# Opening of a two-layer DiT kernel: first scale and constants on other DMA queues, chunks loaded in pairs, modulation columns by transposes and a VectorE sum

## The chip, the cores and the metric

The kernel runs on one core of a Trainium2 chip. The time is the device time of one execution in microseconds; lower is better. All arithmetic is in float32, with matrix products made of three passes over a high and a low part of each operand (`hi` and `lo`, type fp32r).

## The reference, cut to what matters

```python
silu_c, silu_cc = jax.nn.silu(c), jax.nn.silu(c_ctx)
# layer 0
mod   = silu_c  @ ada_w[0] + ada_b[0]        # [1, 6*1024]
mod_c = silu_cc @ ada_w[0] + ada_b[0]
sh1, sc1, g1, sh2, sc2, g2 = jnp.split(mod, 6, axis=-1)     # sh1c, sc1c, ... likewise
h  = x   * (1.0 + sc1)  + sh1                # x:   256 tokens x 1024
hc = ctx * (1.0 + sc1c) + sh1c               # ctx: 256 tokens x 1024
p  = h @ ret_w_in[0]                         # [1024, 6144]: q, k, v, gates of 4 heads; hc likewise
# ... retention over h and hc, layer norms, MLP 1024 -> 4096 -> 1024, then a second layer
# with neighbourhood attention; the output is x, 256 x 1024
```

Only the first step concerns us: the two vectors `sh1` and `sc1` (and those of the context) come from a product with the first 2048 columns of `ada_w[0]`, and only with them can x and ctx be modulated and projected.

## The kernel before, in words

The opening works in eight **chunks** of 128 channels (k = 0 to 7). For chunk k it needs 128 columns of `ada_w[0]` for the shift (i = 0) and 128 for the scale (i = 1), each [1024 x 128], 512 KB, in rows of 512 B; the 128 columns of x and of ctx, 128 KB each, in rows of 512 B; and 128 rows of `ret_w_in[0]` for the q of head 0 (256 columns, 128 KB) and its v (512 columns, 256 KB). `chunk_loads(k)` issues them all on the SyncE queue (SP), in this order. The tile names in the trace are `rawq` (ada_w), `R` (x and ctx) and `raw` (weights).

For each chunk:
- `chunk_sums(k, i)`: TensorE multiplies the ada_w columns by the silu columns `cT`; the sums of eight row blocks land in four groups of 32 partitions of a PSUM bank (`pada`), in two accumulating rounds.
- `chunk_turn(k)`: TensorE transposes the four 128x128 tiles of x and ctx (`pt`, and the second half of the `pada` bank).
- `ws[k].high()`: ScalarE makes the high part of the weights; `ws[k].low()`: VectorE makes the low part.
- `chunk_row(k)`: VectorE copies the sums to SBUF (`row`).
- `chunk_columns(k)`: two float32 matmuls with a selector (`sel4`) add the four partial rows and turn them into columns; VectorE adds the bias (`mod`).
- `chunk_modulate(k)`: ScalarE and VectorE write the modulated high part `hTh`, then the unrounded value `aff`; VectorE subtracts to get the low part `hTl`.
- `chunk_q` and `part_v`: TensorE accumulates q (`pq`) and v (`pv`) over the chunks: 18 matmuls of 512 columns a chunk.

The loop of round k prepares chunk k+1 while it multiplies chunk k. TensorE, VectorE and ScalarE run in the order written out by hand here (their `on` flag is set before the first `turn_over`), and SP always does. So the order on each engine is the order of the code: in round k TensorE does the q and v products with `hTh` of chunk k, the sums and transposes of k+1, `part_v(k, 1, 0)` with `hTl`, the columns of k+1, and `part_v(k, 0, 1)`. From chunk 4 on, `low()` stands ahead of the columns on VectorE; before that, it stands between the two halves of `chunk_modulate`.

Beside the chunks, decay tables are made. In round 0, SP loads the distance table `dt` (192 KB) behind the chunks that were issued before the loop; in round 1 GpSimd makes three variants of it (`strip_tables`); and in rounds 2 to 5, behind `chunk_modulate`, `make_strip` puts four Exp on ScalarE and three operations on VectorE (tiles `e` and `strips`).

Ahead of all that, `turn_over(n)` issues n dummy matmuls (256 columns, operand `still`) that keep TensorE busy. `first_columns` transposes the 16 rows `crow` (c and c_ctx) with the identity in `cst0`, takes silu and spreads the result into `cT`; `first_biases` turns the bias rows `brow0`.

The order ahead of the loop:

```python
    turn_over(16)
    first_columns()
    turn_over(3)
    chunk_sums(0, 0)
    ...
    turn_over(1)
    first_biases()
    turn_over(3)
    chunk_sums(0, 1)
```

Arena slots: `AQ` names four slots of 8 KB a partition, one for each of the chunks in flight (both ada parts of a chunk share one slot). Weights of a chunk lie in a pool of four buffers.

Of the kernel before, what the change touches and what calls it, by code (L numbers as in the profile page):

```python
# [10 lines left out]
F32 = mybir.dt.float32  # L11
F32R = mybir.dt.float32r
AF = mybir.ActivationFunctionType
ALU = mybir.AluOpType
# [3 lines left out]
P = 128  # L18
D = 1024
KC = D // P  # L20
# [84 lines left out]
def kernel(  # L105
# [23 lines left out]
    pe, act, dve, pool, sp = (  # L129
        InOrder(tc, getattr(nc, e), e in PIN)  # L130
        for e in ("tensor", "scalar", "vector", "gpsimd", "sync")
    )
# [19 lines left out]
    def nm(s):  # L152
        uid[0] += 1
        return f"{s}_{uid[0]}"

    def bank(s="ps"):
        return psp.tile([P, 512], F32, tag="ps", name=nm(s))

    def slot(i, shape, dt, s):

        return arena.tile(shape, dt, tag=f"s{i}", name=nm(s))

    def scr(s, dt=F32):
        return scp.tile([P, 512], dt, tag="scr", name=nm(s))

    def tsl(t):
        return slice(t * P, (t + 1) * P)
# [125 lines left out]
    NC0 = P + 4  # L293
    cst0 = cpool.tile([P, NC0], F32, tag="cst0", name="cst0")
    cst1 = cpool.tile([P, CONSTS.shape[1] - NC0], F32, tag="cst1", name="cst1")
    crow = scr("crow")[:, :P]
    brow0 = scr("brow0")[:, :P]
    sp.dma_start(out=crow[0:8, :], in_=c.rearrange("a (k p) -> (a k) p", p=P))
    act.dma_start(out=crow[8:16, :], in_=c_ctx.rearrange("(k p) -> k p", p=P))
    act.dma_start(out=cst0[:], in_=consts[:, 0:NC0])  # L300
    act.dma_start(out=brow0[0:16, :], in_=ada_b[0][0 : 2 * D].rearrange("(r p) -> r p", p=P))

    def cv(name, p0=0, p1=P):
        o, w = CONST_COLS[name]
        if o < NC0:
            return cst0[p0:p1, o : o + w]
        return cst1[p0:p1, o - NC0 : o - NC0 + w]

    ident = cv("ident")
# [4 lines left out]
    bcol = cpool.tile([P, 2, KC], F32, tag="bcol", name="bcol")  # L314
# [4 lines left out]
    def first_columns():  # L319

        pc = bank("pc")
        pe.transpose(pc[:, 0:16], crow[0:16, :], ident[0:16, 0:16])
        act.activation(out=scol[:].rearrange("p a k -> p (a k)"), in_=pc[:, 0:16], func=AF.Silu)
        for t in range(2):
            dve.tensor_copy(
                out=cT[:, :, :, t], in_=scol[:, t, :].unsqueeze(2).broadcast_to([P, KC, 16])
            )

    def first_biases():

        pc = bank("pc")
        pe.transpose(pc[:, 0:16], brow0[0:16, :], ident[0:16, 0:16])
        for a in range(2):
            dve.tensor_scalar_add(out=bcol[:, a], in0=pc[:, 8 * a : 8 * a + 8], scalar1=float(a))

    def ln_rows():
        rows = scr("rows")[:, :P]
        sp.dma_start(out=rows[0:32, :], in_=ln_g.rearrange("l i (k p) -> (l i k) p", p=P))
        sp.dma_start(out=rows[32:64, :], in_=ln_b.rearrange("l i (k p) -> (l i k) p", p=P))
        for i, (l, w) in enumerate(COLUMNS):  # L340
            sp.dma_start(
                out=rows[64 + 16 * i : 80 + 16 * i, :],
                in_=ada_b[l][3 * w * D : (3 * w + 2) * D].rearrange("(r p) -> r p", p=P),
            )
        return rows
# [21 lines left out]
    mods = {}  # L367
# [353 lines left out]
    AQ = (S_GS, S_SH, S_SL, S_VH)  # L721
    adas, ws = {}, {}

    def chunk_ada(k):

        raw = slot(AQ[k % 4], [P, 2, KC, P], F32, "rawq")
        for i in range(2):
            w_ap = ada_w[0][:, i * D + P * k : i * D + P * k + P]
            sp.dma_start(out=raw[:, i], in_=w_ap.rearrange("(k p) n -> p k n", p=P))
        adas[k] = lambda i, kk: raw[:, i, kk, :]  # L730

    def chunk_x(k):
        cols = tsl(k)
        for a, src in enumerate((x, ctx_in)):
            sp.dma_start(out=RR[a][:, :, cols], in_=src[0][:, cols].rearrange("(t p) c -> p t c", p=P))

# [21 lines left out]
    def chunk_loads(k):  # L758
        chunk_ada(k)
        chunk_x(k)  # L760
        ws[k] = Weights(k)

    def turn_over(n):
        for _ in range(n):
            pe.matmul(pq[0][:, :256], lhsT=still[:, :P], rhs=still[:, :256], start=True, stop=True)
# [42 lines left out]
    prs, pts, rows = {}, {}, {}  # L808

    def chunk_sums(k, i):  # L810

        if k not in prs:
            prs[k] = bank("pada")
        for kk in range(KC):
            j = kk % 4
            pe.matmul(
                prs[k][32 * j : 32 * j + 32, tsl(i)],
                lhsT=cT[:, kk, :, :].rearrange("p a t -> p (a t)"),
                rhs=adas[k](i, kk),
                start=(kk < 4),  # L820
                stop=(kk >= 4),
                tile_position=(0, 32 * j),
            )

    def chunk_row(k, cols=slice(0, 2 * P)):
        if cols.start == 0:
            rows[k] = smp.tile([P, 256], F32, tag="row", name=nm("row"), bufs=1)
        dve.tensor_copy(out=rows[k][:, cols], in_=prs[k][:, cols])

    def chunk_columns(k):  # L830
        for i in range(2):
            pe.matmul(
                prs[k][:, 2 * i : 2 * i + 2], lhsT=rows[k][:, tsl(i)], rhs=cv("sel4")[:, 0:2],
                start=True, stop=True,
            )
        dve.tensor_add(
            out=mods[0, 0][:, :, k, :],
            in0=prs[k][:, 0:4].rearrange("p (s t) -> p s t", s=2),
            in1=bcol[:, :, k].unsqueeze(2).broadcast_to([P, 2, 2]),
        )  # L840
# [3 lines left out]
    def chunk_turn(k, ts=range(4)):  # L844

        if k not in pts:
            pts[k] = bank("pt")[:, 0:256], (prs[k][:, 256:512] if k else bank("pt")[:, 0:256])
        for t in ts:
            pe.transpose(pts[k][t // 2][:, tsl(t % 2)], R[t][:, tsl(k)], ident)
# [18 lines left out]
    def chunk_q(k, parts=((0, 0), (1, 0), (0, 1))):  # L868
        w, h = (ws[k].hi, ws[k].lo), hs(k, 0, NT)
        for a, b in parts:  # L870
            for dc in range(2):
                pe.matmul(
                    pq[dc][:], lhsT=w[a][:, tsl(dc)], rhs=h[b],
                    start=(k == 0 and a == b), stop=(k == KC - 1 and b == 1),
                )

    def part_v(k, a, b):
# [4 lines left out]
                start=(k == 0 and a == b), stop=(k == KC - 1 and b == 1),  # L882
            )

    act.dma_start(
        out=lgn[:, 0], in_=ret_decay[0].rearrange("(o d) h -> o (d h)", o=1).broadcast_to([P, 8])
    )
    for k in range(4):
        chunk_loads(k)
    for e in (act, dve, pe):  # L890
        e.on = True
    turn_over(16)
    first_columns()
    turn_over(3)
    chunk_sums(0, 0)
    chunk_row(0, tsl(0))
    turn_over(1)
    first_biases()
    turn_over(3)
    chunk_sums(0, 1)  # L900
    chunk_row(0, tsl(1))
    chunk_turn(0, (0, 1))
    chunk_columns(0)
    chunk_turn(0, (2, 3))
    turn_over(3)
# [9 lines left out]
    for k in range(KC):  # L915
        if k == 0:
            dt = slot(S_VL, [P, 4, 384], F32, "dt")
            sp.dma_start(out=dt[:, 0], in_=dist)
        if k == 3:
            sp.dma_start(out=cst1[:], in_=consts[:, NC0:])  # L920
            lrows = ln_rows()
        if k:
            chunk_q(k, ((0, 0),))
            part_v(k, 0, 0)
            chunk_q(k, ((1, 0), (0, 1)))
        if k < KC - 1:
            for i in range(2):
                chunk_sums(k + 1, i)
            chunk_turn(k + 1)
            ws[k + 1].high()  # L930
            chunk_row(k + 1)
            if k > 2:
                ws[k + 1].low()
        if k < 4:
            chunk_loads(k + 4)
        part_v(k, 1, 0)
        if k < KC - 1:
            chunk_columns(k + 1)
            chunk_modulate(k + 1, lambda: None if k > 2 else ws[k + 1].low())
        part_v(k, 0, 1)  # L940
        if k == 1:
            tabs = strip_tables(dt)
        if 1 < k < 6:
            make_strip(k - 2, *tabs)
        if k == KC - 1:
            ln_columns(lrows)
        if k > 5:
            take(0, 2 * (k - 5))
# [56 lines left out]
    for h in range(RH):  # L1005
# [9 lines left out]
        else:  # L1015
# [15 lines left out]
            for u in range(4):  # L1031
                ((wh, wl),) = take(1)
                for t in range(4):
                    for kk in range(2):
                        k = 2 * u + kk
# [72 lines left out]
        for t in range(4):  # L1108
            po = bank("po")
            scs = list(range(4)) if t < 2 else [2, 3]  # L1110
            for i, sc in enumerate(scs):
                a, b = S[sc]
# [5 lines left out]
            r = rstd_of(mv)  # L1118
            on = scr("on")[:] if t < 2 else gs[:, t, :]
            dve.tensor_scalar(  # L1120
                out=on, in0=po[:], scalar1=mv[:, 0:1], scalar2=r[:], op0=ALU.subtract, op1=ALU.mult
# [155 lines left out]
    for hf in range(2):  # L1277
# [65 lines left out]
        for half in range(2):  # L1343
# [39 lines left out]
            def settle(t):  # L1383

                add_to(t, 1, gated(pb[t], t, 1, G2), dve)
                stat(t, 1)
                return moments(t)
# [14 lines left out]
            m = settle(0)  # L1402
# [5 lines left out]
            m = settle(1)  # L1408
            mm2(2, 4, held[0])
            p = turn(0)  # L1410
# [7 lines left out]
            m = settle(2)  # L1418
            mm2(3, 4, held[0])
            p = turn(1)  # L1420
# [299 lines left out]
    m = settle(3)  # L1720
# [123 lines left out]
    n = NS - 1  # L1844
# [373 lines left out]
```

## Time and profile before

| | before |
|---|---|
| median of 3 runs | 1178.11 us |
| lowest, highest | 1176.97, 1178.76 us |
| the profiled execution | 1180.28 us |
| its span | 1178.2 us |
| TensorE busy in the span | 1168.4 us (99%) |
| VectorE, ScalarE, GpSimd busy | 846.6, 482.0, 212.9 us |
| granted TensorE clock, mean | 0.998 |

The span runs from the first to the last instruction of the profiled execution; 2.1 us of its time lie around it. Busy time of TensorE counts overlapping matmuls as one stretch, so 99% says that TensorE almost always had a matmul in flight, not that it ran at its peak. All times in the lines of the profile are microseconds from the span's start, unless marked ns. A line of the timeline gives the start, the time until the group's end, the engine (PE is TensorE's matmul, PEld its weight load, DVE VectorE, ACT ScalarE, POOL GpSimd, SP SyncE; a q behind the name is the engine's sequencer, which issues DMAs), the source line (here always that of the helper that records operations), the operation, and output tile <- input tiles with shapes and count. In square brackets is the time that the engine stood idle before it, and what ended that time.

### The profile page before, as it was taken

The numbers are of one execution on the slowest core, as the hardware profiler recorded it, in microseconds if no ns is written. First come the engines' busy times: TensorE is split into PE (matmuls) and PEld (weight loads), VectorE is DVE, ScalarE is ACT, GpSimd is POOL, SyncE is SP. The second block draws the span as 40 slices with busy tenths as digits, with TensorE's granted clock in tenths as the row PEclk, the third lists the DMA queues.
The fourth block names the chain that finished last, engine by engine and source line by source line (L and its number), as shares of the span: only waits on it lengthen the run. The fifth ranks groups of instructions, "written<-read, shape, count | busy, mean of one in ns | idle before, by whom it ended". The sixth has DMA issues, their size and how long they took to land.

```text
span 1178.2 us, 17591 instructions
## 1 busy us (share of the span) xinstructions
PE 1168.4 (99%) x6743; PEld 985.0 (84%) x6743; DVE 846.6 (72%) x1351; ACT 482.0 (41%) x819; POOL 212.9 (18%) x364
## 2 busy tenths in 40 slices
PE   9999999999999999999999999999999999999997
PEld 7788888888888889888888888889888878999886
DVE  3887677777888787757767675678576688876446
ACT  3643332232323246341113332137466576665341
POOL 0103001000200241770203000223344430000001
PEclk9999999999999999999999999999999999999999
DMA  9942544544355426756556665647244434765661
GB/s 279 273 143 93 158 146 146 156 144 143 126 170 170 149 59 218 184 110 212 179 183 211 202 207 187 192 140 212 76 144 126 123 123 151 224 197 189 230 213 38
DMA packets 140115, 195.10 MB, mean 166 GB/s; under 512 B 9936, under 2 KB 81136, under 8 KB 140032
## 3 DMA queue, kind: packets, MB, share of 16 engines
q1 hardware_dynamic: 131904, 182.03, 49.6%
q0 software_dynamic: 6976, 9.39, 3.9%
q10 hardware_dynamic: 1152, 2.56, 0.8%
q8 instruction: 53, 0.87, 0.3%
q14 instruction: 30, 0.25, 0.1%
HBM read 189.12 MB, written 5.75 MB: 165 GB/s over the span
## 4 chain that ended last, share of the span: by engine, by line
PE 97%; DVE 1%; ACT 1%; issue 0%; DMA 0%; POOL 0%; DVEq 0%; ACTq 0%
PE p L84 44%; PE pq L84 8%; PE pv L84 8%; PE pg L84 7%; PE pw L84 7%; PE pn L84 5%; PE pnv L84 4%; PE po L84 3%; PE ppt L84 2%; PE pnw L84 1%; PE pS L84 1%; PE pav L84 1%; PE pada L84 1%; PE pqk L84 1%; PE pt L84 1%; PE p1t L84 1%
## 5 line engine op out<-in xcount | busy, mean ns | idle before, releaser
L84 ACT CAST hi<-raw 128x1024 fp32r<-128x1024 f32 (+2 forms) x228 | 232.7, 1032 | 310.9 <-PE p L84 124.3
L84 DVE TENSOR_TENSOR lo<-raw,hi 128x1024 fp32r<-128x1024 f32 (+2 forms) x228 | 274.0, 1213 | 106.2 <-ACT hi L84 105.7
L84 PE MATMUL p<-hi,hid 128*128 128x512 f32 (+1 forms) x780 | 239.0, 386 | 0.0
L84 PEld LDWEIGHTS p<-hi,hid 128*128 128x128 f32 x780 | 145.7, 188 | 29.5
L84 PE MATMUL p<-hTh,lo 128*128 128x256 f32 (+1 forms) x512 | 166.9, 329 | 0.0
L84 PE MATMUL p<-hTl,hi 128*128 128x256 f32 (+1 forms) x512 | 166.9, 329 | 0.0
L84 PE MATMUL p<-hTh,hi 128*128 128x256 f32 (+1 forms) x512 | 164.0, 330 | 0.0
L84 PE MATMUL p<-lo,hid 128*128 128x512 f32 (+1 forms) x390 | 150.5, 386 | 0.0
L84 DVE SCALAR_TENSOR_TENSOR acc<-rawa,scol,acc 128x1024 f32<-128x1024 f32 x56 | 74.6, 1342 | 65.5 <-DMA rawa<-in_ada_w_dram 65.5
L84 PEld LDWEIGHTS p<-hTh,lo 128*128 128x128 f32 x512 | 96.4, 188 | 8.8
L84 PEld LDWEIGHTS p<-hTl,hi 128*128 128x128 f32 x512 | 96.5, 188 | 8.6
L84 PEld LDWEIGHTS p<-hTh,hi 128*128 128x128 f32 x512 | 95.1, 190 | 8.7
L84 PEld LDWEIGHTS p<-lo,hid 128*128 128x128 f32 x390 | 73.3, 188 | 14.5
L84 DVE SCALAR_TENSOR_TENSOR strips<-rawa,scol,strips 128x512 f32<-128x512 f32 x112 | 78.6, 762 | 0.0
L84 ACT CAST hid<-r 128x256 fp32r<-128x256 f32 (+1 forms) x64 | 31.9, 500 | 106.9 <-DVE r L84 106.9
L84 POOL TENSOR_TENSOR rstd<-rstd,misc 128x1 f32<-128x1 f32 x28 | 19.1, 685 | 213.6 <-DVE rstd L84 212.6
L84 POOL TENSOR_TENSOR R<-R,acc 128x512 f32<-128x512 f32 x16 | 25.9, 1635 | 169.8 <-DVE acc L84 169.7
L84 ACT ACTIVATE s<-s,mn 128x512 f32<-128x512 f32 x64 | 45.5, 713 | 22.0 <-DVE mn L84 22.0
L84 PE MATMUL pw<-hi,oh 128*128 128x512 f32 x128 | 51.0, 398 | 0.0
L84 PE MATMUL pg<-hi,hTh 128*128 128x512 f32 x128 | 50.6, 395 | 0.0
L84 PE MATMUL pw<-hi,ol 128*128 128x512 f32 x128 | 50.0, 390 | 0.0
L84 PE MATMUL pg<-hi,hTl 128*128 128x512 f32 x128 | 49.9, 390 | 0.0
(238 smaller groups left out, 2279.8 us busy)
## 6 DMA issues: line engine op xcount, KB each, us to landing
raw<-in_mlp_w_dram SPq DMA_DIRECT2D x128, 512.0 KB, 4.4
rawa<-in_ada_w_dram SPq DMA_DIRECT2D x80, 512.0 KB, 3.9
raw<-in_ret_w_in_dram SPq DMA_DIRECT2D x42, 512.0 KB, 4.0
raw<-in_nat_w_in_dram SPq DMA_DIRECT2D x24, 512.0 KB, 4.5
rawq<-in_ada_w_dram SPq DMA_DIRECT2D x16, 512.0 KB, 6.1
raw<-in_ret_w_o_dram SPq DMA_DIRECT2D x16, 512.0 KB, 3.5
bias<-rpb_rows POOLq DMA_DIRECT2D x32, 128.0 KB, 2.9
raw<-in_nat_w_o_dram SPq DMA_DIRECT2D x8, 512.0 KB, 3.9
```

The lines of the kernel that those rows point to most:

```text
L84: r = f(*args, **kwargs)
```

## The change

Four things are done:
1. The second ada part of chunk 0 (the scale) is issued on the ScalarE queue, and the c_ctx rows behind it on the same queue. The constants, the first bias rows and the decay parameters go to the GpSimd queue.
2. Chunks 0, 1 and 2 are loaded singly as before. Chunks 3 and 4, and 5 and 6, are loaded in pairs: each ada part of a pair is one DMA of 1 MB in rows of 1024 B, x and ctx of a pair are one DMA each of 256 KB, and the weights follow, chunk by chunk. Both shifts of a pair take one arena slot and both scales another. Chunk 7 is loaded singly. The order on SP is chunk 0, 1, 2, pair 3 and 4, `dt`, pair 5 and 6, the later constants, chunk 7.
3. The dummy matmuls become 11, 5, 1 and 2 (and 3 further on, as before).
4. From chunk 1 on, `turned_columns` takes the place of `chunk_columns`: two TensorE transposes of the row into the first half of the `pada` bank, a VectorE reduce that adds the four partial columns, and a VectorE add of the bias in place.

```diff
-    act.dma_start(out=crow[8:16, :], in_=c_ctx.rearrange("(k p) -> k p", p=P))
-    act.dma_start(out=cst0[:], in_=consts[:, 0:NC0])
-    act.dma_start(out=brow0[0:16, :], in_=ada_b[0][0 : 2 * D].rearrange("(r p) -> r p", p=P))
+    pool.dma_start(out=cst0[:], in_=consts[:, 0:NC0])
+    pool.dma_start(out=brow0[0:16, :], in_=ada_b[0][0 : 2 * D].rearrange("(r p) -> r p", p=P))
...
+    def ada_part(i, k, n, out_ap, eng=sp):
+        w_ap = ada_w[0][:, i * D + P * k : i * D + P * (k + n)]
+        eng.dma_start(out=out_ap, in_=w_ap.rearrange("(k p) n -> p k n", p=P))
+
     def chunk_ada(k):
-        raw = slot(AQ[k % 4], [P, 2, KC, P], F32, "rawq")
+        raw = slot(AQ[min(k, 3)], [P, 2, KC, P], F32, "rawq")
         for i in range(2):
-            w_ap = ada_w[0][:, i * D + P * k : i * D + P * k + P]
-            sp.dma_start(out=raw[:, i], in_=w_ap.rearrange("(k p) n -> p k n", p=P))
+            ada_part(i, k, 1, raw[:, i], act if i and k == 0 else sp)
         adas[k] = lambda i, kk: raw[:, i, kk, :]
 
-    def chunk_x(k):
-        cols = tsl(k)
+    def pair_ada(k):
+        raws = [slot(AQ[(k + i) % 4], [P, KC, 2 * P], F32, "rawq") for i in range(2)]
+        for i in range(2):
+            ada_part(i, k, 2, raws[i][:])
+        for a in range(2):
+            adas[k + a] = lambda i, kk, a=a: raws[i][:, kk, tsl(a)]
+
+    def chunk_x(k, n=1):
+        cols = slice(P * k, P * (k + n))
...
+    def pair_loads(k):
+        pair_ada(k)
+        chunk_x(k, 2)
+        for a in range(2):
+            ws[k + a] = Weights(k + a)
...
+    def turned_columns(k):
+        for i in range(2):
+            pe.transpose(prs[k][:, tsl(i)], rows[k][:, tsl(i)], ident)
+        m = mods[0, 0][:, :, k, :]
+        dve.tensor_reduce(
+            out=m, in_=prs[k][:, 0:256].rearrange("p (s j a t) -> p a s t j", s=2, j=4, t=2)[:, 0],
+            axis=mybir.AxisListType.X, op=ALU.add,
+        )
+        dve.tensor_add(out=m, in0=m, in1=bcol[:, :, k].unsqueeze(2).broadcast_to([P, 2, 2]))
...
-    act.dma_start(
+    pool.dma_start(
         out=lgn[:, 0], in_=ret_decay[0].rearrange("(o d) h -> o (d h)", o=1).broadcast_to([P, 8])
     )
-    for k in range(4):
+    for k in range(3):
         chunk_loads(k)
+        if k == 0:
+            act.dma_start(out=crow[8:16, :], in_=c_ctx.rearrange("(k p) -> k p", p=P))
...
-    turn_over(16)
+    turn_over(11)
     first_columns()
-    turn_over(3)
+    turn_over(5)
     chunk_sums(0, 0)
     chunk_row(0, tsl(0))
     turn_over(1)
     first_biases()
-    turn_over(3)
+    turn_over(2)
     chunk_sums(0, 1)
+    pair_loads(3)
...
-        if k < 4:
-            chunk_loads(k + 4)
+        if k == 1:
+            pair_loads(5)
+        if k == 3:
+            chunk_loads(7)
         part_v(k, 1, 0)
         if k < KC - 1:
-            chunk_columns(k + 1)
+            turned_columns(k + 1)
```

## The prediction

> **What bounds the kernel now.** I read the page first (span, busy time, the chain of work that ended last), then the timeline of the first 60 us for all engines, then the DMA issues with their times to landing in narrow windows.
>
> ```profile
> span 1178.2 us, 17591 instructions
> ...
> PE 1168.4 (99%) x6743; PEld 985.0 (84%) x6743; DVE 846.6 (72%) x1351; ACT 482.0 (41%) x819; POOL 212.9 (18%) x364
> ...
> PE 97%; DVE 1%; ACT 1%; issue 0%; DMA 0%; POOL 0%; DVEq 0%; ACTq 0%
> ```
>
> TensorE (PE) has a matmul in flight 99% of the time and holds 97% of the chain. So a microsecond that TensorE loses in the opening is not given back later, and only what moves TensorE counts. But a share of busy time hides short stalls: in the opening TensorE goes at the pace of others, as the next rows show.
>
> Around chunks 3 and 4 (round 2 and the start of round 3):
>
> ```profile
> 25.45 0.55 POOL L84 TENSOR_SCALAR lgn<-lgn 128x8 f32<-128x8 f32 x2 [24.42 <-ACT lgn L84]
> 27.17 0.83 ACT L84 CAST hi<-raw 128x768 fp32r<-128x768 f32 x1 [1.82 <-DMA raw<-in_ret_w_in_dram]
> 27.28 0.38 PE L84 MATMUL pada<-cst,R 128*128 128x128 f32 x2
> 27.73 4.25 POOL L84 TENSOR_SCALAR dt<-dt 128x384 f32<-128x384 f32 x3 [1.54 <-DMA dt<-in_dist_dram]
> 28.43 0.50 PE L84 MATMUL pada<-cst,row 128*128 128x2 f32 x4
> 28.97 0.16 DVE L84 TENSOR_TENSOR mod<-pada,bcol 128x4 f32<-128x4 f32 x1 [0.84 <-PE pada L84]
> 29.17 0.56 ACT L84 ACTIVATE hTh<-pt,mod 128x256 fp32r<-128x256 f32 x1 [1.17 <-DVE mod L84]
> 30.27 1.71 ACT L84 ACTIVATE e<-dt,lgn 128x384 f32<-128x384 f32 x3
> 32.40 0.56 DVE L84 TENSOR_TENSOR strips<-e,dt 128x384 f32<-128x384 f32 x1
> 32.88 0.55 DVE L84 TENSOR_TENSOR strips<-e,e 128x384 f32<-128x384 f32 x1
> 34.25 0.42 DVE L84 COPY row<-pada 128x256 f32<-128x256 f32 x1 [0.82 <-PE pada L84]
> ```
>
> Two things are to be seen. The weights of chunk 3 are used as they land: ScalarE idles 1.82 us for them and starts at 27.17. And `dt` is used as it lands: GpSimd starts at 27.73, ends three operations at 31.98, and the VectorE add that reads the third (`strips<-e,dt`) starts at 32.40, 0.42 us later. VectorE works in the code's order, so that add stands ahead of the row copy of chunk 4 at 34.25, with only 0.82 us of idle time between. Together, `dt` may be late by some 1.2 us before TensorE feels it.
>
> The pace of the later chunks:
>
> ```profile
> 45.21 1.08 PE L84 MATMUL pada<-rawq,cT 128*32 128x128 f32 x32
> 46.91 0.42 DVE L84 COPY row<-pada 128x256 f32<-128x256 f32 x1 [0.86 <-PE pada L84]
> 47.26 0.95 DVE L84 TENSOR_TENSOR lo<-raw,hi 128x768 fp32r<-128x768 f32 x1
> 47.64 0.50 PE L84 MATMUL pada<-cst,row 128*128 128x2 f32 x4
> 48.00 1.16 PE L84 MATMUL pv<-lo,hTh 128*128 128x512 f32 x4
> 48.18 0.16 DVE L84 TENSOR_TENSOR mod<-pada,bcol 128x4 f32<-128x4 f32 x1
> 48.37 0.57 ACT L84 ACTIVATE hTh<-pt,mod 128x256 fp32r<-128x256 f32 x1 [2.19 <-DVE mod L84]
> 49.03 0.30 PEld L84 LDWEIGHTS pq<-hTh,hi 128*128 128x128 f32 x2 [0.30 <-ACT hTh L84]
> 51.55 0.48 PEld L84 LDWEIGHTS pada<-rawq,cT 128*32 128x32 f32 x20 [0.37 <-issue]
> ```
>
> A chunk takes 51.55 - 45.21 = 6.34 us. The `mod` add has no idle time before it: VectorE comes to it straight from `lo`, which ends at 48.21, while the columns of TensorE end at 48.14. From there a chain runs without a gap: `mod`, ScalarE's `hTh`, and TensorE's next weight load, which waited for `hTh`.
>
> **The change part by part.** *Opening.* The rows of before:
>
> ```profile
> 0.74 0.58 ACTq L84 DMA_DIRECT2D crow<-in_c_ctx_dram  x1
> 1.20 1.03 SPq L84 DMA_DIRECT2D rawq<-in_ada_w_dram  x2
> 1.23 3.79 PE L84 MATMUL pq<-still 128*128 128x256 f32 x16 [1.23 <-DVE still L84]
> 4.95 0.28 PE L84 MATMUL pc<-cst,crow 16*128 16x16 f32 x1
> 6.10 0.70 PE L84 MATMUL pada<-rawq,cT 128*32 128x128 f32 x16
> 7.75 0.65 PE L84 MATMUL pada<-rawq,cT 128*32 128x128 f32 x16
> ...
> rawq<-in_ada_w_dram SPq DMA_DIRECT2D x2, 512.0 KB, 5.2
> cst<-in_consts_dram ACTq DMA_DIRECT2D x1, 66.0 KB, 3.5
> ...
> gate<-in_ada_b_dram POOLq DMA_DIRECT2D x4, 4.0 KB, 3.3
> lns<-lsc POOLq DMA_DIRECT2D x1, 32.0 KB, 4.8
> ```
>
> `first_columns` (4.95) now starts when the 16 dummies end and the constants land (issue 1.36 + 3.5). After: the constants go out on GpSimd at about 0.75; the nearest rows of that queue land 3.3 us (a bias row) to 4.8 us (`lns`, under load) after issue, so at 4.0 to 5.5. The c_ctx rows go out behind 512 KB of the scale on the same queue; the `rawq` pair takes 5.2 us to land, so they may land as early as 3 (if small rows overtake) or as late as 0.75 + 5.2 = 5.9. The bounds for `first_columns` are thus 4.0 and 5.9, against 4.95. The first 512 KB starts 0.46 us earlier (0.74 instead of 1.20), and the scale no longer queues behind the shift on SP (its sums ran at 7.75, those of the shift at 6.10). I take zero for TensorE's start of chunk 1, with -1.0 and +0.9 as ends: what hides it either way is the wait in the next part. The stream of loads I take as 0.5 us earlier (that start), with 0 and 1.0 as ends. GpSimd's three issues cost nothing: its first work here was at 25.45 (the `lgn` scaling, then `dt`), and SP has fewer issues than before (six a chunk, eight a pair).
>
> *Pairs.* All loads of the chunks run through one queue without a pause, and `dt` stands in it. Its place moves from behind chunk 3 to behind chunks 3 and 4.
>
> ```profile
> 22.89 0.43 SPq L84 DMA_DIRECT2D dt<-in_dist_dram x1
> ...
> dt<-in_dist_dram SPq DMA_DIRECT2D x1, 192.0 KB, 4.8
> ...
> GB/s 290 302 355 333 316 317 277 292 300 293 298 341 338 324 294 293 291 290 290 293 316 361 355 328 307 289 292 289 313 284 324 327 335 308 297 292 294 287 277 312
> ...
> GB/s 369 396 382 355 360 346 341 346 355 350 355 351 346 387 364 391 382 364 337 100 100 64 91 218 273 373 400 364 273 128 27 18 0 0 0 0 64 109 127 209
> ```
>
> The first GB/s line is 12 to 36 us in slices of 0.6 us, the second 51 to 60 us, where only weights in 2 KB rows move. The plateaus near 292 are ada_w in 512 B rows; the peaks of 330 to 361 are the weights in rows of 1 and 2 KB, and 2 KB rows alone reach 340 to 390. For rows of 1 KB I take 350, the middle of those peaks (ends 292 and 370).
>
> Before, `dt` lands at 22.89 + 4.8 = 27.7. From the end of chunk 2's loads to there stood 1.31 MB in 512 B rows (4.5 us at 292) and 0.59 MB of weights and `dt` (1.6 us at 360): 6.1 us. After, there stand two chunks, 2 x 1.70 MB, and 0.20 MB of `dt`, 3.60 MB at 350: 10.3 us. So `dt` lands 4.2 us later, less 0.5 for the earlier start: 3.7 us later, at 31.4.
>
> Then, from the rows above: GpSimd's three operations take 4.25 and end at 35.7; the add reads the third at 35.75, the next strip follows 0.48 later and lasts 0.55, and the row copy of chunk 4 comes at 36.8 instead of 34.25: **+2.5 us**. TensorE's columns need that row. The chunk's own data are late too: chunk 3's weights land ahead of chunk 4's (0.39 MB, 1.1 us) and `dt` (0.56), so at 29.7; the cast takes 0.83, and `hTh`, behind it on ScalarE, starts at 30.6 instead of 29.17. That is +1.4 and lies inside the +2.5; it is also what swallows the opening, which would have to gain or lose more than that to be seen. Pair 5 and 6 is due 9 us after `dt`, at some 41 for the last weights of chunk 6, which TensorE wants after 48; chunk 7 likewise is hidden.
>
> *Columns.* Out go four matmuls of 0.36 us on TensorE (47.64 to 48.00); in come two transposes, 0.11 apart and over after 0.38 (27.28, `pada<-cst,R` x2). On VectorE one add becomes a reduce and an add that waits for it. No row shows that reduce; the nearest are these small operations:
>
> ```profile
> L84 DVE TENSOR_TENSOR mod<-pada,acol 128x16 f32<-128x16 f32 x6 | 1.0, 167 | 0.4 <-PE pada L84 0.4
> L84 DVE TENSOR_SCALAR nmr<-mv,rstd 128x1 f32<-128x1 f32 x10 | 2.1, 210 | 2.4 <-POOL rstd L84 2.3
> ```
>
> I take 0.17, the row of the same 16 elements from PSUM, and 0.03 until the add: 0.20 (ends 0.15 and 0.25; not below 0.15, since an added instruction of VectorE stands in a chain without idle time). In chunks 4 to 7 `lo` holds VectorE until 48.21, so the columns' earlier end buys nothing and `mod` comes 0.20 later, four times: **+0.8 us**. In chunks 1 to 3 the transposes end 0.1 earlier and the reduce costs 0.2; that is +0.1 each, hidden by the waits of chunks 3 and 4. If VectorE had slack, TensorE would gain 0.25 a chunk: that is a rival below.
>
> The sum: +2.5 + 0.8 = +3.3 us, of 1178.2 us of span, or 1183.6 against the profiled execution's 1180.28. That execution lies 2.2 us over the median of the three runs, so the time is 1178.11 + 3.3 = **1181.4 us**. With `dt` between 30.3 (370 GB/s, stream 1.0 earlier) and 32.6 (320 GB/s, 0.5), the forecast's own range is 1180.1 to 1182.8.
>
> **The rivals.**
> *Loads in time, no change.* If the stream is ahead by more than I think, so that `dt` lands by 28.9 (27.7 and the 1.2 us of slack), neither wait appears. For it: two queues and fewer, larger DMAs at the start; the first 10 us hold small rows that moved to another queue. Against it: 1.7 MB more stand ahead of `dt`, and at 350 they need 4.9 us. Then the columns stay at +0.8 and +0.3, the opening at some -0.5: +0.6, 1178.7.
>
> *TensorE is the bound, faster.* If TensorE's own work is what counts, as the chain's 97% says, the place is its instruction stream ahead of and in the chunks: four dummies fewer at 0.22 (16 in 3.79) and 0.25 less for each of seven columns, 0.9 + 1.7 = 2.6 us, 1175.5. It decides if `dt` lands by 28.9 and `mod` ends no later than now, that is if the reduce and the add take under 0.2 together. Against it: `mod` has no idle time before it at 48.18.
>
> *Pairs bring no rate, slower still.* If rows of 1 KB move at the 292 of 512 B rows, the 3.60 MB need 12.3 us, `dt` lands at 33.4, and the sum is +5.3: 1183.4. The Trainium skill's page "DMA: Bandwidth & Descriptors", section "Specifications", puts the least row for full rate at 512 B, by which doubling it brings nothing and the time would be this one. By that rule no difference should show between 512 B and 2 KB rows, but the trace has 292 against 340 to 390, so I give it little.
>
> **How the numbers follow.** My forecast has 0.50, loads in time 0.25, TensorE as the bound 0.10, no rate 0.10; 0.05 is left for the opening being late by more than the waits swallow. Faster or slower means by over 0.2%, 2.4 us, about what a measurement of this kernel can tell from no change; that bound, 1180.5, cuts the lower part of my forecast, about 0.12 of its 0.50. So faster has 0.10 (the second rival); same 0.25 + 0.12 + 0.02 = 0.39; slower 0.38 + 0.10 + 0.03 = 0.51. The range from 1177.5 to 1183.6 takes in the first rival with an opening better by 1 us, my forecast and most of the third; it leaves out the second and the worst of the third, some 0.15.
>
> **What would show it.** Right: GpSimd's `dt` operations start at 31 to 32 instead of 27.73; VectorE's `strips<-e,dt` waits for GpSimd, and ScalarE's second `e` too; the row copy of chunk 4 stands near 36.8; ScalarE's cast of chunk 3 waits for DMA until 29.7; a later chunk takes 6.5 us instead of 6.34, with TensorE waiting longer for `hTh`. Wrong: `dt` landing before 29, a chunk time of 6.34 or less, or a reduce that overlaps `lo`. What happens after 60 us I expect unchanged; a moved instruction order there would also break the sum.

## The result and the profile after

The kernel after takes 1184.28 us (median of 6 runs, 1183.77 to 1185.48), the kernel before 1178.38 in its runs beside them (6 runs): 1.0053 times as long, interval 1.0043 to 1.0064. It is slower by 5.9 us. The forecast was +3.3, and 1184.28 lies above its range.

The page of the kernel after:

```profile
span 1182.1 us, 17561 instructions
...
PE 1168.1 (99%) x6725; PEld 982.1 (83%) x6725; DVE 846.9 (72%) x1358; ACT 480.1 (41%) x819; POOL 214.8 (18%) x367
```

TensorE's busy time is that of before (1168.4), so the loss does not show in this line. Two things hide it: matmuls at half pace count as busy too, and in the profiled execution of the kernel before a stretch of the second layer's MLP went slower with the same instructions. From one of its matmuls (start at 1004.14 before, 1010.88 after) to a later one (1096.10 and 1099.88) that stretch took 91.96 us before and 89.00 after. That is also why the profiled spans differ by 3.9 us only. So the stages are compared here by their start, not by the span.

The opening on TensorE after, from the timeline:

```profile
1.23 2.72 PE L84 MATMUL pq<-still 128*128 128x256 f32 x11 [1.23 <-DVE still L84]
6.82 0.28 PE L84 MATMUL pc<-cst,crow 16*128 16x16 f32 x1 [2.88 <-DMA cst<-in_consts_dram]
...
8.40 1.08 PE L84 MATMUL pada<-rawq,cT 128*32 128x128 f32 x16
...
10.87 1.08 PE L84 MATMUL pada<-rawq,cT 128*32 128x128 f32 x16
...
16.48 1.91 PE L84 MATMUL pv<-hi,hTh 128*128 128x512 f32 x4
18.18 1.05 PE L84 MATMUL pq<-hTl,hi 128*128 128x512 f32 x2
19.17 1.08 PE L84 MATMUL pada<-rawq,cT 128*32 128x128 f32 x32
```

And the row of before that answers to the last one:

```profile
12.91 1.08 PE L84 MATMUL pada<-rawq,cT 128*32 128x128 f32 x32
```

Two things are to be seen. First, `first_columns` starts at 6.82 instead of 4.95, after 2.88 us of idle time that ended with the constants. Second, the pace: both times the 16 sums of chunk 0 take 1.08 us (0.70 and 0.65 before), and its four `pv` products 1.91 (1.08 before). So TensorE worked at half its pace there. Chunk 1's sums, twice as many, take 1.08 us as they did before: by 19.17 the full pace is back. Chunk 1 starts 6.26 us late, of which `first_columns` explains 1.87.

The issue of the constants after, from the timeline, and then the DMA issues of the first 3.4 us (KB each, and the time from issue to landing in us):

```profile
1.29 0.75 POOL L84 DMA_DIRECT2D cst<-in_consts_dram  x1 [0.84 <-POOLq L2235]
```

```profile
rawq<-in_ada_w_dram ACTq DMA_DIRECT2D x1, 512.0 KB, 4.0
rawq<-in_ada_w_dram SPq DMA_DIRECT2D x1, 512.0 KB, 5.3
...
cst<-in_consts_dram POOLq DMA_DIRECT2D x1, 66.0 KB, 5.5
```

The 66 KB of constants were issued at 1.29 and needed 5.5 us on GpSimd's queue, longer than the 512 KB beside them. On ScalarE's queue, issued at 1.36, they had needed 3.5 before.

Later chunks after, chunk 3 to chunk 5, from the timeline:

```profile
31.88 0.55 POOL L84 TENSOR_SCALAR lgn<-lgn 128x8 f32<-128x8 f32 x2 [28.55 <-ACT lgn L84]
...
32.60 4.24 POOL L84 TENSOR_SCALAR dt<-dt 128x384 f32<-128x384 f32 x3
...
39.12 0.56 DVE L84 TENSOR_TENSOR strips<-e,dt 128x384 f32<-128x384 f32 x1
...
39.26 1.08 PE L84 MATMUL pada<-rawq,cT 128*32 128x128 f32 x32
...
41.30 0.95 DVE L84 TENSOR_TENSOR lo<-raw,hi 128x768 fp32r<-128x768 f32 x1
...
42.17 0.17 DVE L84 TENSOR_REDUCE mod<-pada 128x4 f32<-128x16 f32 x1
...
45.74 1.08 PE L84 MATMUL pada<-rawq,cT 128*32 128x128 f32 x32
```

`dt` was issued at 24.89 and landed 7.0 us later, at 31.9, about as late as forecast (31.4). But nobody waits for it any more, because the whole stream of chunks is over 6 us late itself: GpSimd waits for ScalarE's `lgn` until 31.88 and comes to `dt` without a pause, at 32.60, and the row of `strips` has no bracket. A chunk takes 45.74 - 39.26 = 6.48 us, 0.14 more than the 6.34 of before.

### The profile page after: what moved, and what is told of

Same layout as the page of the kernel before. It is cut to its first block, busy times and chain, and to the rows that moved or that the text cites. A ratio compares the mean times of both kernels' runs of the same rounds, so it can differ in the third digit from the quotient of the medians.

```text
span 1182.1 us, 17561 instructions
## 1 busy us (share of the span) xinstructions
PE 1168.1 (99%) x6725; PEld 982.1 (83%) x6725; DVE 846.9 (72%) x1358; ACT 480.1 (41%) x819; POOL 214.8 (18%) x367
## 4 chain that ended last, share of the span: by engine, by line
PE 96%; ACT 1%; DVE 1%; issue 1%; DMA 0%; DVEq 0%; ACTq 0%; POOLq 0%
PE p L84 44%; PE pq L84 8%; PE pw L84 7%; PE pg L84 7%; PE pv L84 7%; PE pn L84 5%; PE pnv L84 4%; PE po L84 3%; PE pnw L84 2%; PE ppt L84 2%; PE pS L84 1%; PE pav L84 1%; PE pqk L84 1%; PE pada L84 1%; PE pt L84 1%; PE p1t L84 1%
## 5 line engine op out<-in xcount | busy, mean ns | idle before, releaser
L84 ACT CAST hid<-r 128x256 fp32r<-128x256 f32 (+1 forms) x64 | 31.9, 500 | 111.2 <-DVE r L84 111.2
L84 PE MATMUL pq<-hTh,hi 128*128 128x512 f32 x128 | 49.9, 400 | 2.0 <-ACT hTh L84 1.9
```

What stands on the lines that cost most here:

```text
L84: r = f(*args, **kwargs)
```

## The experiments

Each is compared with runs of the kernel before on the same chip. "Chunk 1 starts" is the start of its sums on TensorE in the profile, 12.91 before.

| run | what | median us | before | ratio, interval | chunk 1 starts |
|---|---|---|---|---|---|
| e1 | opening alone | 1183.62 | 1177.99 | 1.0050, 1.0038 to 1.0063 | 18.79 |
| e2 | after, 29 dummies | 1182.25 | 1177.99 | 1.0037, 1.0024 to 1.0051 | 14.56 |
| e3 | pairs alone | 1180.70 | 1177.99 | 1.0024, 1.0015 to 1.0033 | 12.75 |
| e4 | columns alone | 1178.12 | 1177.99 | 1.0005, 0.9996 to 1.0013 | 12.80 |
| e5 | pairs alone, table first | 1180.64 | 1177.92 | 1.0021, 1.0012 to 1.0030 | 13.35 |
| e6 | opening, constants first on ScalarE | 1184.20 | 1177.92 | 1.0057, 1.0044 to 1.0070 | 18.84 |
| e7 | opening, 29 dummies | 1179.67 | 1177.92 | 1.0017, 1.0007 to 1.0028 | 14.52 |
| e8 | before, 11 dummies | 1181.22 | 1177.92 | 1.0028, 1.0016 to 1.0039 | 16.89 |
| e9 | before, one pair from chunk 5 | 1180.40 | 1178.71 | 1.0014, 1.0005 to 1.0023 | 17.09 |
| e10 | before, scale on ScalarE | 1183.91 | 1178.71 | 1.0046, 1.0033 to 1.0059 | 16.46 |
| e11 | before, dummies moved | 1177.82 | 1178.28 | 0.9993, 0.9982 to 1.0004 | 12.69 |
| e12 | e9 profiled again | 1183.17 (one run) | 1178.28 | | 12.92 |

### Which part loses the time: e1, e3, e4

e1 takes only parts 1 and 3 of the change into the kernel before (queues and dummies), e3 only the pairs, e4 only the columns:

```diff
# e4, the columns alone
-            chunk_columns(k + 1)
+            turned_columns(k + 1)
```

> The kernel before with the opening's part alone: queues and dummy counts of the changed kernel, single chunks, old columns. Clock theory (the constants land late on the GpSimd queue, TensorE stands idle and then works at half pace): first_columns at about 6.8 us, sums of chunk 1 at about 19.2 instead of 12.91, matmul pace of chunk 0 halved, total +5.5 to +6.5 us (ratio 1.005). Rival, as predicted (opening swallowed by the loads of chunks 3 and 4): chunk 1 at 12 to 14, total within +-1 us.

> The kernel before with the pairs alone: queues, dummy counts and columns of before. Late-table theory of the prediction: dt lands at 31 to 32 instead of 27.7, GpSimd's three operations start there, the row copy of chunk 4 stands at 36.5 to 37.5 instead of 34.25, total +2 to +3 us (ratio 1.002). Rival (loads in time): dt by 28.9, total within +-0.5 us.

> The kernel before with turned_columns alone. VectorE-chain theory: chunks 4 to 7 take 6.34 + 0.14 = 6.48 us, chunks 1 to 3 6.55 + 0.08, total +0.8 us (ratio 1.0007). Rival (TensorE's work is the bound): a chunk 0.25 us shorter, total -1.7 us (ratio 0.9985).

The opening alone loses 5.6 us, nearly all of the 5.9. Its timeline has the half pace, and nothing is given back later:

```profile
8.37 1.08 PE L84 MATMUL pada<-rawq,cT 128*32 128x128 f32 x16
...
18.79 1.08 PE L84 MATMUL pada<-rawq,cT 128*32 128x128 f32 x32
...
57.46 1.08 PE L84 MATMUL pada<-rawq,cT 128*32 128x128 f32 x32
```

Chunk 7 started at 51.55 before: +5.88 at chunk 1, +5.91 at chunk 7. Pairs alone lose 2.7 us and columns alone 0.1, with an interval that reaches from -0.5 to +1.5 us; in its profile chunk 7 starts at 52.33, 0.78 late. The three alone add up to 8.5 us, the change loses 5.9: behind the late opening the pairs are hidden. Each against its own runs of the kernel before, the whole change loses only 0.3 us more than e1.

### Half pace or late constants: e2, e7, e8

e7 is the opening alone, e2 the whole change, both with more dummies ahead of `first_columns`. e8 is the kernel before with fewer:

```diff
# e2 and e7
-    turn_over(11)
+    turn_over(29)
# e8
-    turn_over(16)
+    turn_over(11)
```

> The changed kernel with 29 instead of 11 dummy matmuls ahead of first_columns, so that TensorE stays busy until the constants land at 6.8 us. Clock theory: first_columns still at 6.8 to 7.2, but chunk 0 at full pace, chunk 1 at about 15 instead of 19.17, and then the wait for the distance table shows (row copy of chunk 4 at about 37.3 instead of 40.96): total 2.5 to 3.5 us under the changed kernel, about +3 us over the kernel before. Rival (only the late constants count, the pace does not matter): chunk 1 stays above 18.5 and the total within 1 us of the changed kernel's, +6.

> The opening alone, with 29 dummy matmuls instead of 11 ahead of `first_columns`, so that TensorE has no idle time before the constants land; single chunks, columns as before. Theory of the pace: `first_columns` near 7.0, sums of chunk 0 take 0.64 us for 16, chunk 1 starts at 14.4 to 14.7 (12.91 before, 18.79 with the opening alone), nothing more is lost after it (chunks of 6.55 and 6.34 as before): +1.5 to +1.8 us, 1179.5 to 1179.8. Rival (the new order of the loads costs by itself, beyond the constants): chunk 1 starts after 15.5 or a later chunk waits for its loads, 1181 or more.

> The kernel before with 11 dummies instead of 16 ahead of `first_columns`, nothing else: the constants land on time (4.8 us), TensorE is idle for about 0.9 us before them. Theory that any break in the dummies starts the pace over: `first_columns` at 4.95, sums of chunk 0 at 1.08 us for 16, half pace until 12 us or later, chunk 1 at 15 to 17.5 instead of 12.91, 1180 to 1182.5. Rival (a break under 1 us only delays full pace by as much): full pace by 7 us, chunk 1 at 12.9 to 13.4, 1178.0 to 1178.5.

e7, the timeline of TensorE:

```profile
6.96 0.23 PE L84 MATMUL pc<-cst,crow 16*128 16x16 f32 x1 [0.63 <-DMA cst<-in_consts_dram]
...
7.91 0.65 PE L84 MATMUL pada<-rawq,cT 128*32 128x128 f32 x16
...
14.52 1.08 PE L84 MATMUL pada<-rawq,cT 128*32 128x128 f32 x32
```

The constants are as late as in e1, and even 29 dummies left 0.63 us of idle time, but TensorE keeps the full pace it had reached (16 sums in 0.65), and chunk 1 starts at 14.52 instead of 18.79. e8, the same view:

```profile
4.78 0.26 PE L84 MATMUL pc<-cst,crow 16*128 16x16 f32 x1 [0.84 <-DMA cst<-in_consts_dram]
...
5.91 1.08 PE L84 MATMUL pada<-rawq,cT 128*32 128x128 f32 x16
...
16.89 1.31 PE L84 MATMUL pada<-rawq,cT 128*32 128x128 f32 x32
```

Here every load is on time and `first_columns` starts no later than before. Five dummies fewer and 0.84 us of idle time cost 4 us by chunk 1 and 3.3 us in the median. One profile alone could not show this, since e9 below has such a late full pace with sixteen dummies too; but all six runs of e8 lie from 1180.83 to 1182.11. So the rival, that a short break only delays the full pace by as much, falls, and the opening's loss is divided: 14.52 - 12.91 = 1.6 us for the late inputs, 18.79 - 14.52 = 4.3 us for the half pace.

e2 lost more than e7 (4.3 against 1.75 us) and more than the 3 that were expected of it. With the opening only 1.65 us late the table is waited for again, as its VectorE row shows (0.39 us of idle time ended by GpSimd), and from chunk 4 to chunk 5 it takes 7.99 us instead of 6.3:

```profile
34.90 1.08 PE L84 MATMUL pada<-rawq,cT 128*32 128x128 f32 x32
...
37.18 0.56 DVE L84 TENSOR_TENSOR strips<-e,dt 128x384 f32<-128x384 f32 x1 [0.39 <-POOL dt L84]
...
42.89 1.08 PE L84 MATMUL pada<-rawq,cT 128*32 128x128 f32 x32
```

### Which queue: e6, e10

e6 is the opening alone with the constants ahead of the scale on ScalarE's queue. e10 is the kernel before with only the scale moved (third on ScalarE's queue) and biases and decay on GpSimd:

```diff
# e6, against e1
-    pool.dma_start(out=cst0[:], in_=consts[:, 0:NC0])
+    act.dma_start(out=cst0[:], in_=consts[:, 0:NC0])
# e10, against before
-            sp.dma_start(out=raw[:, i], ...)
+            (act if i and k == 0 else sp).dma_start(out=raw[:, i], ...)
```

> The opening alone, with one thing undone: the constants go out first on ScalarE's queue, ahead of the scale (c_ctx rows stay behind the scale, biases and decay on GpSimd, 11 dummies). Both theories: the constants land by about 4.5 us instead of 6.75, and `first_columns` starts when the c_ctx rows land, at 5.5 to 6.3 instead of 6.79. Theory of the pace (after 11 dummies TensorE stands idle and then works at half pace, whatever it waited for): the idle is still 1.5 to 2.3 us, the sums of chunk 0 still take 1.08 us for 16 matmuls, chunk 1 starts at 17.5 to 18.5 and the time is 1182 to 1183.3. Rival (the constants' landing alone is the loss): chunk 1 starts at 13.5 to 14.5, the time is 1178.5 to 1179.5.

> The part of the opening that leaves TensorE's inputs on time: ScalarE's queue sends c_ctx rows, constants, then the scale; biases and decay go out on GpSimd; 16, 3 and 3 dummies, single chunks and columns as before. The constants land at 4 to 5 us and `first_columns` starts at 4.8 to 5.2. Theory (the loads of chunk 0 are bound by their rate, so their order gives little, but no dummy is missing): chunk 1 starts at 12.4 to 13.1, 1177.4 to 1178.6. Rival 1 (SP's queue, freed of the scale, is worth its 0.5 us and more): chunk 1 at 12.2 or earlier, 1177.3 or less. Rival 2 (the shift now shares the rate with the scale and lands near 6.9 instead of 5.7; TensorE has no dummy left for that gap and falls back to half pace): chunk 1 at 15 to 17.5, 1180.5 to 1182.

e6, the constants' issue, then TensorE:

```profile
cst<-in_consts_dram ACTq DMA_DIRECT2D x1, 66.0 KB, 1.9
```

```profile
7.56 0.26 PE L84 MATMUL pc<-cst,crow 16*128 16x16 f32 x1 [3.61 <-DMA crow<-in_c_ctx_dram]
...
9.11 1.08 PE L84 MATMUL pada<-rawq,cT 128*32 128x128 f32 x16
```

On ScalarE's queue and first in it, the constants need 1.9 us instead of 5.5. But nothing is won: now the 4 KB of c_ctx rows, behind the scale on that queue, are awaited until 7.56, later than both theories had said. So each of the two moves can hold TensorE up. How late the c_ctx rows were in the kernel after, where the constants came last, no row shows: the scale ahead of them needed 4.0 us from its issue there and 6.8 in e6. The half pace is there. Chunk 1 (18.84) and the median (1184.20) came later than the theory of the pace had said; the time is that of e1 within the intervals.

In e10 the constants are on time and there are 16 dummies. The timeline of TensorE, and then the stretches of 4 us from 5 us on: busy time and count of the five engines, then the granted clock (third figure from the end), the DMA share and GB/s:

```profile
5.89 0.64 PE L84 MATMUL pada<-rawq,cT 128*32 128x128 f32 x16
...
8.84 1.08 PE L84 MATMUL pada<-rawq,cT 128*32 128x128 f32 x16 [1.27 <-DMA rawq<-in_ada_w_dram]
```

```profile
5.00:9.00 4.00, 2.70 (x30) 1.93 (x33) 0.89 (x5) 0.18 (x1) 0.00 (x0) 0.97 1.11 252
9.00:13.00 4.00, 3.91 (x28) 3.08 (x24) 1.55 (x5) 1.83 (x4) 0.00 (x0) 0.50 1.18 313
13.00:17.00 4.00, 4.00 (x30) 2.96 (x33) 1.53 (x3) 0.94 (x2) 0.00 (x0) 0.67 1.16 312
17.00:21.00 4.00, 4.00 (x39) 3.17 (x32) 1.96 (x5) 1.13 (x2) 0.00 (x0) 1.00 1.17 314
```

TensorE had reached full pace (16 sums in 0.64). Then the scale, not the shift as the second rival had it, came late, and after 1.27 us of idle time the next 16 sums take 1.08: the granted clock falls to 0.50 and is back at 1.00 only after 15 us. This is the row that says what the half pace is. The median says +5.2 us, more than any of the three expectations. The profile has 3.6 of it by chunk 1 and 1.05 more at 428.11, where TensorE waits 1.29 us for ScalarE's `xn` (0.24 before); why that wait grew is open. So also with the constants on time the scale does not gain from ScalarE's queue.

### What carries the pairs' loss: e5, e9, e12

The timeline of e3, the pairs alone:

```profile
27.82 0.65 PE L84 MATMUL pada<-rawq,cT 128*32 128x128 f32 x16 [1.14 <-DMA rawq<-in_ada_w_dram]
...
29.31 0.44 PE L84 MATMUL pada<-cst,R 128*128 128x128 f32 x2 [0.31 <-DMA R<-in_ctx_dram]
...
29.50 1.90 PE L84 MATMUL pv<-hi,hTl 128*128 128x512 f32 x4
...
32.02 4.63 POOL L84 TENSOR_SCALAR dt<-dt 128x384 f32<-128x384 f32 x3 [5.80 <-DMA dt<-in_dist_dram]
...
32.28 0.56 ACT L84 ACTIVATE hTh<-pt,mod 128x256 fp32r<-128x256 f32 x1 [1.05 <-DVE mod L84]
...
36.68 0.56 DVE L84 TENSOR_TENSOR strips<-e,dt 128x384 f32<-128x384 f32 x1 [0.38 <-POOL dt L84]
...
37.62 0.42 DVE L84 COPY row<-pada 128x256 f32<-128x256 f32 x1
```

The signs that the prediction named are there: GpSimd's `dt` at 32.02, the `strips` that wait for it, the row copy late (37.62 instead of 34.25). But TensorE also waits for chunk 3's own scale and ctx rows, and `hTh` of chunk 3 stands at 32.28 instead of 29.17, 3.1 us late without any help of the table.

These 3.1 us are not the loads' waits alone. Behind the waits of 1.14 and 0.31 us TensorE fell to half pace once more: the four `pv` products at 29.50 take 1.90 us, 1.17 in e5 at the same place. The granted clock of the stretch (third figure from the end) says so:

```profile
28.00:33.50 5.50, 5.09 (x33) 3.92 (x26) 1.80 (x4) 1.98 (x4) 1.48 (x2) 0.69 1.08 358
```

If the clock was either 1.00 or 0.50 there, 0.69 means some 3.4 us at half pace. e5 sends the table ahead of the pair:

```diff
# e5, against e3
+    dt = slot(S_VL, [P, 4, 384], F32, "dt")
+    sp.dma_start(out=dt[:, 0], in_=dist)
     pair_loads(3)
...
-            dt = slot(S_VL, [P, 4, 384], F32, "dt")
-            sp.dma_start(out=dt[:, 0], in_=dist)
```

> The pairs alone, but with the distance table `dt` sent ahead of the first pair instead of behind it (0.2 MB of loads pass from behind to in front of chunk 3's own data). With the pairs alone TensorE's chunk 4 sums started at 35.82 us (32.55 before) and the time was 1180.7. Theory of the prediction (the late table carries the loss): `dt` lands near 24 us, GpSimd's three operations start by 26.5 instead of 32.0, the row copy of chunk 4 comes back to 35.0 to 35.7, and of the loss about 1.3 stays (chunk 3's weights): 1179.2 to 1179.6. Rival (chunk 3's own data carry it: its scale part landed at 27.77 and its ctx rows at 29.26 with the pairs alone, and TensorE and VectorE waited for them): everything of chunk 3 lands 0.5 to 0.6 later still, chunk 4's sums start at 36.0 to 36.5, and the time is 1180.7 to 1181.4.

```profile
22.49 4.94 POOL L84 TENSOR_SCALAR dt<-dt 128x384 f32<-128x384 f32 x3 [21.46 <-DMA dt<-in_dist_dram]
...
28.48 0.65 PE L84 MATMUL pada<-rawq,cT 128*32 128x128 f32 x16 [1.39 <-DMA rawq<-in_ada_w_dram]
...
37.00 0.42 DVE L84 COPY row<-pada 128x256 f32<-128x256 f32 x1 [0.82 <-PE pada L84]
```

The table is used at 22.49 and nobody waits for it, and yet the row copy of chunk 4 stands at 37.00, 2.75 us later than before: two waits lay side by side, and taking one away left the other. In this profile 0.44 of the 2.75 are a later opening (chunk 1 at 13.35); the other 2.3 come between chunk 1 and chunk 4, where TensorE waits for chunk 3's own loads. In e3 the row copy stands 1.80 behind chunk 4's first sums (37.62 and 35.82), in e5 1.71 (35.29): in that profile of e3 the table added 0.1.

The median, 1180.64, is that of e3, but that equality is partly chance. Four of the ten runs of e5, the profiled one among them, took 1179.56 to 1179.95 with a mean granted clock of 0.999. The other six took 1180.56 to 1181.73, five of them with 0.996 or 0.997, like the profiled run of e3 (0.996) with its fall to half pace. Only the profiled run has a trace, so a fall in those five is inferred from the clock alone. In e3 ten of the eleven runs have 0.998 or 0.999. So where the clock held, by these few runs, the pairs cost about 2.0 us with the table ahead and 2.7 with it behind: the chunk's own loads carry most of the loss, and the table some 0.7 of it. Neither expectation holds whole: the row copy did not come back to 35.7, and chunk 4 started at 35.29, ahead of the 36.0 that the rival had said.

e9 makes a pair only of chunks 5 and 6:

```diff
# e9, against before
-        if k < 4:
-            chunk_loads(k + 4)
+        if k == 0:
+            chunk_loads(4)
+        if k == 1:
+            pair_loads(5)
+        if k == 3:
+            chunk_loads(7)
```

> The kernel before, with the loads of chunks 5 and 6 alone made a pair (sent once chunk 2's sums are done); chunks 0 to 4 and 7 are loaded singly, the distance table stands behind chunk 3, opening and columns as before. Theory (a pair costs only where TensorE needs its first chunk at once): the data of chunk 5 land by 40 us and are wanted after 45, so nothing waits; chunk 4 starts at 32.4 to 32.7, later chunks take 6.34, 1177.7 to 1178.4. Rival (a pair costs by itself, through larger transfers or the slots it fills): TensorE waits for a load between chunks 4 and 7, +1 us or more, 1179 or more.

> The same kernel as the pair from chunk 5, profiled once more. Its first profile had chunk 0 at half pace (chunk 1 at 17.09 us) and a wait of 1.92 us for weights at 776 us, and was the slowest of its runs. Theory (the half pace was that execution's, the later wait is the pair's doing): chunk 1 at 12.8 to 13.4, a wait of about 2 us between 60 and 1000 us, 1179.6 to 1180.7. Rival (nothing of it is the pair's): no such wait, 1177.5 to 1178.5. Rival 2 (half pace is usual for this kernel): chunk 1 near 17, 1182 or more.

The median says +1.7 us, where the theory had none. The first profile could not show why, because that execution was at half pace all through chunk 0, although its opening is that of before and its first rows are the same to 0.01 us:

```profile
4.94 0.28 PE L84 MATMUL pc<-cst,crow 16*128 16x16 f32 x1
...
6.10 1.08 PE L84 MATMUL pada<-rawq,cT 128*32 128x128 f32 x16
...
17.09 1.29 PE L84 MATMUL pada<-rawq,cT 128*32 128x128 f32 x32
```

With everything 4.2 us late the pair of chunk 5 was in time. The second profile (e12) had full pace, and shows the wait:

```profile
39.97 0.64 PE L84 MATMUL pada<-rawq,cT 128*32 128x128 f32 x16 [0.21 <-DMA rawq<-in_ada_w_dram]
...
42.50 0.83 ACT L84 CAST hi<-raw 128x768 fp32r<-128x768 f32 x1 [3.13 <-DMA raw<-in_ret_w_in_dram]
...
47.56 1.08 PE L84 MATMUL pada<-rawq,cT 128*32 128x128 f32 x32
```

From chunk 5 (39.11) to chunk 6 it takes 8.45 us instead of 6.34: +2.1, the same kind of loss as at chunk 3. My expectation had chunk 5's data wanted after 45; its sums are due in round 4, at 39. The theory that a pair costs where its first chunk is wanted at once holds, with a date that I had wrong. The wait that I had expected after 60 us, from e9's first profile, did not come again. e12's single time, 1183.17, lies above what was expected of it; in its profile the stretch of the second layer's MLP took 91.96 us, as in the profile of the kernel before, and 89.2 in e9's.

### Can the opening of before be made safer: e11

```diff
# e11, against before
     first_columns()
-    turn_over(3)
+    turn_over(6)
...
     first_biases()
-    turn_over(3)
+    turn_over(1)
```

> The kernel before with three of its dummies, in number two moved and one more, placed earlier: 16, then 6 (instead of 3) behind `first_columns`, later 1 (instead of 3) behind the biases. In two of the profiles so far whose opening was that of the kernel before, TensorE reached full pace late (at 7.2 us with the table first, at 17 with the pair from chunk 5), in the others at about 6. Theory (16 dummies make a busy stretch so short that full pace hangs on where it falls): a longer unbroken stretch of full-size matmuls holds full pace by 7 us in the profile, chunk 1 at 12.9 to 13.4, the median at 1177.4 to 1178.2 and no run near 1181.5, where some runs of the kernel before lie. Rival (the late full pace has another cause): the median is the same or higher by the moved dummies (0.3), with runs near 1181.5 as before.

1177.82 against 1178.28 us, interval 0.9982 to 1.0004: not told apart from no change. Full pace held in its profile, and no run lay above 1180.9 us, but twelve runs are too few to say that a late full pace has become rarer. Nor does a time above 1180 us show a late full pace: the profiled execution of the kernel before had it at some 6 us and took 1180.28, its extra time lying in the MLP stretch. No version beat the kernel before beyond its uncertainty.

## Why the prediction was wrong, step by step

**The opening is the step that failed.** The prediction took "zero for TensorE's start of chunk 1, with -1.0 and +0.9 as ends". Measured: +6.26 (e1: +5.88). Two pieces of it were wrong.
- The constants were said to land at 4.0 to 5.5 on GpSimd's queue: issued at about 0.75, and 3.3 to 4.8 us under way by two later rows of that queue. They were issued at 1.29, took 5.5 us beside the first chunk's loads and ended TensorE's wait at 6.82. At full pace the late inputs cost 1.6 us by chunk 1 (e7).
- The dummies were counted as TensorE's own time: five fewer cost nothing, and the rival with a gain even booked four fewer at 0.9 us. What they keep up, the pace, was not in the sum at all; it is 4.3 us of the opening (e1 against e7), and 3.3 us in the median where nothing but the dummies is changed (e8).

The Trainium skill's page "TensorE: Matmul & The Clock Gate", section "What's actually happening", has a rule that speaks to this: TensorE's clock is halved by default and is let go after some 3.4 us of sustained work, in windows that run free of the kernel's start. By it, as an estimate, the eleven dummies (2.72 us by their row) are too few and the sixteen (3.79, with three more behind `first_columns`) just enough. The kernels here agree in the main: none with eleven reached full pace before 17 us; with sixteen it came at some 6 us in most profiles, at 7.2 in e5's and at 17 in e9's. The same section has the clock halved again after an idle window of about 3.4 us. That does not fit e10, where 1.27 us of idle time halved it, nor e3, where waits of 1.14 and 0.31 us did.

**What hides what was the wrong way round.** The opening was to vanish in the wait of chunks 3 and 4. It was larger, so the chunks' waits vanished in the opening: the whole change loses only 0.3 us more than e1.

**The pairs' term had the right size and only part of the cause.** Alone they cost 2.7 us, forecast 2.5; that the sizes agree is luck in part. In e3 `dt` was used at 32.02 (forecast 31.4), and the GB/s of the kernel after from 16 to 26 us, in 40 slices, bear out the 350 taken for 1 KB rows, from the eleventh slice on:

```profile
GB/s 291 289 293 285 291 289 295 299 297 299 322 369 299 338 360 348 365 373 344 369 340 356 365 340 344 356 348 344 348 352 336 352 360 336 348 356 344 336 361 344
```

But of chunk 3's own loads only the weights were followed (+1.4); its scale part and ctx rows, which TensorE takes first, were left out, and by e5 these loads alone cost about 2.0 of the 2.7 us. "Pair 5 and 6 is hidden" held in the kernel after only because all chunks there are late; at the pace of before such a pair costs 2.1 us (e12).

**The columns** cost 0.14 us a later chunk instead of 0.20, with the reduce at the 0.17 that was taken. The reduce overlaps `lo` by 0.08 in the record, which the prediction had named as a sign of being wrong. From chunk 1 to chunk 7 the delay grows from 6.26 to 7.13, by 0.9, where +0.8 was forecast; in e4's profile, from -0.11 to +0.78, it grows as much. This agreement too is luck in part: half of the 0.9 arises before chunk 4 (6.71 late there), where the prediction had +0.1 a chunk and took it as hidden. Of the gain that TensorE as the bound would have made (1175.5), the columns' 1.7 us are excluded by e4's interval and the dummies' 0.9 by e8.

**The rivals.** None of the three came. What came is the 0.05 left for "the opening being late by more than the waits swallow".

## What to carry to other kernels

Dummy matmuls are there to bring TensorE to full pace: count them by the unbroken time until then with a margin (sixteen failed once here, in e9), let them reach to the landing of the inputs, and price a missing microsecond of them by the half pace of all that follows (here 4 us). When a small transfer changes its queue, price its landing beside everything that starts with it, not by rows of that queue at a quiet time. A pair of loads delays its first half by the time of the second (here some 2 us where the first half is wanted at once): follow every load of the first consumer, for two waits may lie side by side. And a wait of TensorE for loads can cost more than its length, when the pace falls behind it.

## What the runs showed of the hardware

- The granted clock is not to be trusted at the start: in the kernel after it reads 1.00 in every stretch from 1 to 21 us, although 16 sums take 1.08 us there. In e10, where TensorE falls back from full pace, it reads 0.50. In the opening the durations tell the pace, the clock row does not.
- TensorE at half pace stayed there for long while busy: in e8 from 4.78 to some 17 us, with matmuls in flight 3.9 to 4.0 of every 4 us from 5 us on. Full pace came 2 to 5 us after the long products (512 columns) of chunk 0 had begun. What the small matmuls and transposes before them lack is not settled here.
- Once full pace is reached, the length of a break alone does not say whether it lasts: a break of 0.63 us (e7) and the two of 1.39 and 0.32 us (e5) left it, one of 1.27 us (e10) and the two of 1.14 and 0.31 us (e3) ended it.
- The same opening reached full pace at some 6 us (before, e3, e4, e12), at 7.2 (e5) or 17 (e9). How often the late cases come in the kernel before was not measured.
- A 4 KB load behind 512 KB on the same queue was awaited until 7.56 us (e6), and the 66 KB of constants took 1.9 us first on ScalarE's queue, 3.5 second on it and 5.5 on GpSimd's. The Trainium skill's page "DMA: Bandwidth & Descriptors", section "Latency and other measured facts", has the first byte of a load after about 1 us from GpSimd and after about 0.6 us from the other queues, by which, as an estimate, 0.4 us lie between them; the 2 us and more seen here are not explained by that, and what else held the constants back was not tried.
